# A hybrid decoder trunk on one core: the RWKV chunk inverse kept in SBUF, its blocks moved by 32 by 32 transposes on VectorE and joined on TensorE, and one norm's two partial sums in the other order

## The chip, the cores and the metric

The kernel runs on one core of one Trainium2 chip. The metric is device time in microseconds (us) of one execution. TensorE is called PE here, VectorE DVE, ScalarE ACT, GpSimd POOL; SP is the engine that issues most DMAs. PE's clock has two levels, 1.2 and 2.4 GHz; a granted clock of 1.00 in a row is the upper one.

## The reference, cut to what matters

The model has two layers. Each is a half-step SwiGLU network ("FFN0"), a mixer of three parallel branches, and a second half-step SwiGLU ("FFN2"); a normalisation and a modulation by a conditioning vector stand ahead of each. Everything is float32, with 256 tokens and a width of 1024.

```
for l in range(2):
    u = modulate(rms_norm(h, norm_w[l, 0]), m[0], m[1])
    h = h + 0.5 * m[2] * swiglu(u, ffn_w_gate[l, 0], ffn_w_up[l, 0], ffn_w_down[l, 0])
    u = modulate(rms_norm(h, norm_w[l, 1]), m[3], m[4])
    p = u @ w_in[l]            # attention | RWKV-7 | HGRN2 | gates
    y = g_a*(diff_attention(..) @ w_out_a) + g_b*(rwkv7_time_mix(..) @ w_out_b) + g_c*(hgrn2_mix(..) @ w_out_c)
    h = h + m[5] * (y @ w_out)
    (FFN2 as FFN0, with m[6..8])

# RWKV-7, per head (8 heads of 64), token after token:
s_kk  = state @ kk_t
state = state * w_t - outer(s_kk, kk_t * a_t) + outer(v_t, k_t)
out_t = state @ r_t
```

The kernel computes the RWKV recurrence in chunks of 64 tokens. For each of 8 heads and 4 chunks that needs the inverse of a unit triangular 64 by 64 matrix, whose off-diagonal part stands in `H`: 32 inverses in each layer. They are built up from blocks: 16 by 16 diagonal blocks by substitution, then the off-diagonal blocks of 32 by 32, then those of 64 by 64.

## The kernel before, in words

**The stream of weights.** All weights are streamed once, in items of up to 512 KB, by DMAs that SP issues (`raw`). ACT rounds each item to `wh` (L375), DVE makes the remainder `wl = raw - wh` (L376), and PE multiplies three products, wh·uh, wh·ul and wl·uh, in `mm3` (L372) or, for the token-major projections, in `tm_proj` (L952 to L954). Each of `wh` and `wl` has three buffers, and an item's matmuls stand two items behind its split.

**The side work.** RWKV, HGRN2 and attention work is written as generators ("tracks"). Between two items `advance` steps them until the costs that they yield use up the item's budget (a negative yield ends the item's share). A scheduler with priorities (`PRIO`) then makes each engine's fixed order from that. So the side work of every engine stands in one queue with the split of the weights: an instruction of the inverse that takes long on DVE stands ahead of a `wl`, and PE waits for that.

**The inverse**, `rwkv_rest`, once a layer. GpSimd issues DMAs that move the 32 by 32 diagonal blocks from `H` to DRAM (`scrA`) and back as `NT`, one block to a partition: 64 of them, stored twice. Fifteen steps t = 1..15 on DVE (L799, L801) make row t of the inverse `Y` of two 16 by 16 blocks at a time. The off-diagonal 16 by 16 block of each follows in four DVE instructions over 2048 elements a partition (L808, L811, L813, L816), half of the eight-row stripes in partitions 0 to 63, half in 64 to 127. `Y` goes back through DRAM (`scrY`) to `Ys`, and the off-diagonal 32 by 32 blocks of the 64 by 64 matrices are made on PE: `Xa` is a transpose on DVE (L837), 32 matmuls (L841), ACT copies to `Tt` (L843), 32 matmuls (L847), DVE copies to `Ys` (L849). The chunk loop behind it (L859 on) reads `Ys`. HGRN2's levels (L1016 to L1078) wait for the flag `inv`, which this function sets.

**Startup.** Before the first item, `mod_step` makes the modulation one column of 128 after another (DVE L324, `mw`), and from it `zf` (ACT L1366, DVE L1367), its split `zh`, `zl` (ACT L375, DVE L376) and the first matmuls (PE L1376). The first step of the generator `constants` is taken there; its other steps come between items.

**Norm sums.** `z_sums` adds the squares of eight tiles of `h` over partitions: GpSimd has summed the squares of all tiles but the last into `acc` (L422), the last stands in `sq`, and PE multiplies `acc` and then `sq` by ones into one PSUM tile (L433).

Of the kernel before, what the change touches and what calls it, by code (L numbers as in the profile page):

```python
# [10 lines left out]
F32 = mybir.dt.float32  # L11
# [3 lines left out]
AF = mybir.ActivationFunctionType  # L15
# [48 lines left out]
def trunk(ctx: ExitStack, tc: tile.TileContext, A, out):  # L64
# [36 lines left out]
    id32 = cp.tile([128, 32], F32, name="id32")  # L101
    omu = cp.tile([128, L, 15], F32, name="omu")
# [21 lines left out]
    def constants():  # L124
# [26 lines left out]
        for i, n in enumerate(LV):  # L151
# [9 lines left out]
            for r in range(0, 128, 32):  # L161
                GP.tensor_copy(lmask[r:r + 32, i], lmf[r:r + 32, 1, r:r + 32])
            yield 0.1
# [265 lines left out]
    def z_sums():  # L429
        ps = psm([128, 2])  # L430
        for i, sq in enumerate((NOW["acc"], NOW["sq"])):
            for b in range(2):
                PE.matmul(ps[:, b:b + 1], sq[:, b * 128:(b + 1) * 128], ones[:, 0:1],  # L433
                          start=i + b == 0, stop=i + b == 2)
# [114 lines left out]
    scr = drp.tile([2, 2, 16, 32, 32], F32, name="scrA")  # L549
    scy = drp.tile([2, 2, 16, 32, 32], F32, name="scrY")  # L550
# [3 lines left out]
    def mixer(l):  # L554
# [218 lines left out]
        def rwkv_rest():  # L773
# [5 lines left out]
            for q in range(2):  # L779
                for p in range(2):  # L780
                    r0 = 64 * p + 32 * q
# [5 lines left out]
            for d in range(2):  # L787
                GP.dma_start(NT[64 * d:64 * d + 64], scr.rearrange("q p m s t -> (q p m) s t"))
            GP.memset(Y, 0.0)
            GP.memset(Y.rearrange("m a b -> m (a b)")[:, 0:1024:33], 1.0)  # L790
            yield 0.1
# [5 lines left out]
            for t in range(1, 16):  # L797
                tm = TM[:, 0:2 * t * t].rearrange("m (g j s) -> m g j s", g=2, j=t)
                V.tensor_tensor(tm, ap(Y, 0, [[528, 2], [32, t], [1, t]]), ap(NT, t, [[528, 2], [0, t], [32, t]]),  # L799
                                ALU.mult)  # L800
                V.tensor_reduce(ap(Y, t, [[528, 2], [32, t]]), tm, AX.X, ALU.add)  # L801
                yield 0.2 + 4 * t * t / 960.0
            Yh = tile_([128, 8, 16], "Yh", "rnt")
            PT = tile_([128, 8, 16], "PT", "rny")
            V.tensor_copy(Yh[0:64], Y[0:64, 0:8, 0:16])
            V.tensor_copy(Yh[64:128], Y[64:128, 8:16, 0:16])
            tm = TM.rearrange("m (j t s) -> m j t s", j=8, t=16)
# [5 lines left out]
            V.tensor_tensor(tm, PT.unsqueeze(2).to_broadcast([128, 8, 16, 16]),  # L813
                            ap(Y, 528, [[0, 8], [1, 16], [32, 16]]), ALU.mult)
            yield 2.2
            V.tensor_reduce(Yh, tm, AX.X, ALU.add)  # L816
            yield -2.2
            V.tensor_copy(Y[0:64, 0:8, 16:32], Yh[0:64])
            V.tensor_copy(Y[64:128, 8:16, 16:32], Yh[64:128])
            sm = scy.rearrange("q p m s t -> (q p m) s t")  # L820
            GP.dma_start(sm[:, 0:8], Y[0:64, 0:8])
            GP.dma_start(sm[:, 8:16], Y[64:128, 8:16])
# [647 lines left out]
```

## Time and profile before

| | |
|---|---|
| runs shown | 1449.04, 1449.73, 1454.76 us; median 1449.73 |
| the profiled execution | 1454.69 us, of which the span of the profile is 1453.0 |
| mean granted clock of PE over the span | 0.988 |
| PE busy | 1401.6 us, 96% |
| DVE busy | 1184.9 us, 82% |
| ACT busy | 803.3 us, 55% |
| POOL busy | 150.2 us, 10% |

The profile follows one execution. It gives for each engine what ran when and, for each idle stretch, which instruction ended it. Waits are put down to the one that came last. "x8" in a timeline row is a run of eight instructions of one form in succession.

### The profile page before, as it was taken

Reading aid. Unit: us, or ns where it says so; the run is one execution under the profiler, and the core shown is the slowest. Engines: PE = TensorE matmul, PEld = TensorE weight load, DVE = VectorE, ACT = ScalarE, POOL = GpSimd, SP = SyncE. Lnnn points to the kernel's source line nnn. Section 1 sums busy time; section 2 is a strip of 40 time slices with the busy share of each in tenths; the row PEclk is TensorE's granted clock in tenths of the full one; section 3 lists DMA queues with packets and bytes.
Section 4 is the critical chain, followed back from the end, with each engine's and each line's share of the span. In section 5 each row is a group of like instructions: output and inputs, shape, how many; then the busy total and the mean of one; then the engine's idle time right before and its main releaser. Section 6 shows DMA issues by size and latency. Waiting matters only on the chain. (4 is left out here: it accounts for less than half of the span.)

```text
span 1453.0 us, 31223 instructions
## 1 busy us (share of the span) xinstructions
PE 1401.6 (96%) x12420; PEld 1331.2 (92%) x12420; DVE 1184.9 (82%) x2216; ACT 803.3 (55%) x1374; POOL 150.2 (10%) x251
## 2 busy tenths in 40 slices
PE   4999999999899999999999999999989999999999
PEld 3899999998678899999999999999877789999998
DVE  5999988869679999888879898787797788886553
ACT  2575447874255646554545544588534664665542
POOL 6200010031310021000000000100322001100000
PEclk9999999999799999999999999999999999999999
DMA  9769984455415657899878998544552235665564
GB/s 358 264 241 362 322 311 167 146 160 163 130 60 178 201 183 264 291 332 319 303 251 296 351 344 299 191 143 144 182 165 78 76 129 174 202 220 192 198 194 127
DMA packets 90370, 316.51 MB, mean 218 GB/s; under 512 B 10608, under 2 KB 13040, under 8 KB 90224
## 3 DMA queue, kind: packets, MB, share of 16 engines
q1 hardware_dynamic: 86832, 308.84, 62.0%
q0 software_dynamic: 1600, 4.20, 1.1%
q8 instruction: 97, 1.59, 0.4%
q10 hardware_dynamic: 1792, 1.48, 0.4%
q14 instruction: 49, 0.40, 0.1%
HBM read 312.38 MB, written 2.10 MB: 216 GB/s over the span
## 5 line engine op out<-in xcount | busy, mean ns | idle before, releaser
L375 ACT CAST wh<-raw 128x1024 fp32r<-128x1024 f32 (+1 forms) x440 | 455.5, 1036 | 426.9 <-PE psd L372 237.3
L376 DVE TENSOR_TENSOR wl<-raw,wh 128x1024 fp32r<-128x1024 f32 (+1 forms) x440 | 537.2, 1222 | 110.7 <-ACT wh L375 106.6
L372 PE MATMUL psd<-uh,wl 128*128 128x256 f32 x1664 | 228.9, 279 | 6.5 <-DVE wl L376 6.5
L372 PE MATMUL psd<-uh,wh 128*128 128x256 f32 x1664 | 231.4, 280 | 0.0
L372 PE MATMUL psd<-ul,wh 128*128 128x256 f32 x1664 | 227.1, 278 | 0.0
L372 PEld LDWEIGHTS psd<-uh,wl 128*128 128x128 f32 x1664 | 207.2, 189 | 8.2 <-DVE wl L376 7.7
L372 PEld LDWEIGHTS psd<-uh,wh 128*128 128x128 f32 x1664 | 207.7, 188 | 5.0 <-issue 2.7
L372 PEld LDWEIGHTS psd<-ul,wh 128*128 128x128 f32 x1664 | 206.4, 188 | 0.4
L324 DVE SCALAR_TENSOR_TENSOR mw<-mw,cbc 128x1024 f32<-128x1024 f32 x134 | 168.2, 1257 | 1.7 <-DMA mw<-in_modw 1.6
L372 PE MATMUL psd<-hl,wh 128*128 128x256 f32 x704 | 96.8, 278 | 0.0
L372 PE MATMUL psd<-hh,wl 128*128 128x256 f32 x704 | 96.6, 278 | 0.0
L372 PE MATMUL psd<-hh,wh 128*128 128x256 f32 x704 | 96.3, 277 | 0.0
L422 POOL TENSOR_TENSOR acc<-acc,sq 128x256 f32<-128x256 f32 x36 | 31.1, 865 | 575.1 <-ACT sq L420 443.6
L372 PEld LDWEIGHTS psd<-hl,wh 128*128 128x128 f32 x704 | 87.9, 188 | 0.0
L372 PEld LDWEIGHTS psd<-hh,wl 128*128 128x128 f32 x704 | 87.9, 188 | 0.0
L372 PEld LDWEIGHTS psd<-hh,wh 128*128 128x128 f32 x704 | 87.7, 188 | 0.0
L953 PE MATMUL psd<-wl,uh 128*128 128x512 f32 x160 | 66.5, 416 | 3.8 <-DVE wl L376 3.8
L954 PE MATMUL psd<-wh,ul 128*128 128x512 f32 x160 | 67.3, 421 | 0.0
L952 PE MATMUL psd<-wh,uh 128*128 128x512 f32 x160 | 66.0, 414 | 0.0
L372 PE MATMUL psd<-zh,wh 128*128 128x258 f32 x448 | 65.2, 286 | 0.0
L372 PE MATMUL psd<-zh,wl 128*128 128x258 f32 x448 | 64.9, 283 | 0.0
L372 PE MATMUL psd<-zl,wh 128*128 128x258 f32 x448 | 63.9, 283 | 0.0
(428 smaller groups left out, 2032.3 us busy)
## 6 DMA issues: line engine op xcount, KB each, us to landing
raw<-in_gu SPq DMA_DIRECT2D x176, 512.0 KB, 4.7
mw<-in_modw SPq DMA_DIRECT2D x134, 512.0 KB, 5.5
raw<-in_wfm SPq DMA_DIRECT2D x94, 512.0 KB, 3.3
raw<-in_dn SPq DMA_DIRECT2D x64, 512.0 KB, 4.7
raw<-in_wtm SPq DMA_DIRECT2D x40, 512.0 KB, 3.3
raw<-in_dn SPq DMA_DIRECT2D x32, 384.0 KB, 4.4
raw<-in_wo SPq DMA_DIRECT2D x24, 512.0 KB, 3.3
raw<-in_wout SPq DMA_DIRECT2D x16, 512.0 KB, 3.3
```

Source lines behind the costliest of these rows:

```text
L324: ins = V.scalar_tensor_tensor(w, w, 1.0, NOW["cbc"], ALU.mult, ALU.mult, accum_out=modd[:, l, j, f:f + 1])
L372: PE.matmul(p, w[:, sl[k]], xs[k][x], start=first and i == 0, stop=last and i == 3 * n - 1)
L375: SC.copy(dst_h, src)
L376: V.tensor_sub(dst_l, src, dst_h.bitcast(F32))
L422: GP.tensor_add(NOW["acc"], NOW["acc"], sq)
L952: PE.matmul(ps[b], u[k][0][:, ts_], w1, start=k == 0, stop=False)
L953: PE.matmul(ps[b], u[k][0][:, ts_], w2, start=False, stop=False)
L954: PE.matmul(ps[b], u[k][1][:, ts_], w1, start=False, stop=k == KT - 1)
```

## The change

The change keeps the inverse in SBUF and has these parts.

1. `Hd` collects the 32 by 32 diagonal blocks of `H` by four copies (two ACT, two POOL). One DVE transpose of 32 by 32 squares (128x512, `To`) puts each column of a block in a partition, so that with scaling by a mask each of the 128 partitions holds one 16 by 16 block in `NT`.
2. The mask `half` (1 in the partitions of the second halves of the squares, and its complement) is made once, in `constants`, from `lmf`: two DVE instructions in the pass n = 16.
3. The fifteen steps work on one 16 by 16 block a partition, so on t·t elements instead of 2·t·t.
4. A second transpose puts `Y` back, two ACT instructions with the mask make the block-diagonal `Yd`, and a third transpose makes `Xa`. The off-diagonal 16 by 16 blocks are made on PE: two groups of 64 matmuls of 32 by 32, on the four tile positions (32i, 32i), with an ACT copy (`Tt`) between them and a DVE addition behind. Copies (two ACT, two POOL) put the result in `Ys`, and a fourth transpose makes `Xa` for the 64 by 64 step.
5. The 64 by 64 step stays, but its two groups run over m outside and p inside, so that two tile positions alternate.
6. The yield costs differ, and `scrA`, `scrY`, the 2048-element tile and 12 DMAs a layer are gone.
7. `z_sums` multiplies `sq` first and `acc` second.

```diff
+            if n == 16:
+
+                V.tensor_reduce(half[:, 0:1], lmf[:, 1], AX.X, ALU.max)
+                V.tensor_scalar(half[:, 1:2], half[:, 0:1], -1.0, 1.0, ALU.mult, ALU.add)
             yield 0.1
...
-        for i, sq in enumerate((NOW["acc"], NOW["sq"])):
+        for i, sq in enumerate((NOW["sq"], NOW["acc"])):
...
-                    GP.dma_start(scr[q, p].rearrange("m s t -> s m t"),
-                                 H[r0:r0 + 32, :, :, 32 * q:32 * q + 32].rearrange("s j c t -> s (j c) t"))
-            NT = tile_([128, 32, 32], "NT", "r")
-            Y = tile_([128, 32, 32], "Y", "k")
-            TM = hp.tile([128, 2048], F32, name="TM", tag="ZH")
...
+            quad = [slice(32 * i, 32 * i + 32) for i in range(4)]
+            Hd = tile_([128, 16, 32], "Hd", "Xa")
+            for i, r in enumerate(quad):
+                (GP.tensor_copy if i % 2 else SC.copy)(
+                    Hd[r].rearrange("s (j c) t -> s j c t", j=4), H[r, :, :, 32 * (i % 2):32 * (i % 2) + 32])
+            yield -0.1
...
+            To = tile_([128, 16, 32], "To", "Tt")
+            V.transpose(To.rearrange("p t (g m) -> p t g m", g=2), Hd.rearrange("p m (g t) -> p t g m", g=2))
+            GP.memset(Bd[:, :, 0:16], 0.0)
+            SC.activation(Bd[:, :, 16:32], Hd[:, :, 16:32], AF.Copy, scale=half[:, 0:1])
+            yield -0.7
+            SC.activation(NT, To[:, :, 0:16].rearrange("p t s -> p s t"), AF.Copy, scale=half[:, 0:1])
+            V.scalar_tensor_tensor(NT, To[:, :, 16:32].rearrange("p t s -> p s t"), half[:, 1:2], NT, ALU.mult, ALU.add)
+            yield -0.4
...
             for t in range(1, 16):
-                tm = TM[:, 0:2 * t * t].rearrange("m (g j s) -> m g j s", g=2, j=t)
...
-                yield 0.2 + 4 * t * t / 960.0
...
-            V.tensor_tensor(tm, Yh.unsqueeze(2).to_broadcast([128, 8, 16, 16]),
-                            ap(NT, 16, [[0, 8], [1, 16], [32, 16]]), ALU.mult)
-            yield 2.2
-            V.tensor_reduce(PT, tm, AX.X, ALU.add)
-            yield 2.2
...
+                tm = TM[:, 0:t * t].rearrange("m (j s) -> m j s", j=t)
+                V.tensor_tensor(tm, ap(Y, 0, [[16, t], [1, t]]), ap(NT, t, [[0, t], [16, t]]), ALU.mult)
+                V.tensor_reduce(ap(Y, t, [[16, t]]), tm, AX.X, ALU.add)
+                yield 0.4 + 2.7 * t * t / 960.0
+            To = tile_([128, 16, 32], "To", "Tt")
+            V.transpose(To.rearrange("p t (g m) -> p t g m", g=2),
+                        Y.rearrange("p s t -> p t s").unsqueeze(2).to_broadcast([128, 16, 2, 16]))
             M["inv"] = True
-            yield 0.255
-
+            yield -0.7
+            for g in range(2):
+                SC.activation(Yd[:, :, 16 * g:16 * g + 16], To[:, :, 16 * g:16 * g + 16].rearrange("p t m -> p m t"),
+                              AF.Copy, scale=half[:, g:g + 1])
+            yield -0.1
             Xa = tile_([128, 16, 32], "Xa")
             Tt = tile_([128, 16, 32], "Tt")
             p1 = psm([128, 16, 32])
+            V.transpose(Xa, Yd)
+            yield -0.6
+            for m in range(16):
+                for i, r in enumerate(quad):
+                    PE.matmul(p1[r, m], Bd[r, m], Xa[r, m], start=True, stop=True, tile_position=(32 * i, 32 * i))
+            SC.copy(Tt, p1)
+            yield -0.2
+            p2 = psm([128, 16, 32])
+            for m in range(16):
+                for i, r in enumerate(quad):
+                    PE.matmul(p2[r, m], Tt[r, m], Yd[r, m], start=True, stop=True, tile_position=(32 * i, 32 * i))
+            V.tensor_tensor(Yd[:, :, 16:32], Yd[:, :, 16:32], p2[:, :, 16:32], ALU.add)
+            for i, r in enumerate(quad):
+                (GP.tensor_copy if i % 2 else SC.copy)(Ys[r, :, 32 * (i % 2):32 * (i % 2) + 32], Yd[r])
+            V.transpose(Xa, Yd)
+            yield -1.0
...
-            for p, (a_, b_) in enumerate(hv):
-                for m in range(16):
+            for m in range(16):
+                for p, (a_, b_) in enumerate(hv):
                     PE.matmul(p1[b_, m], H[a_, m // 4, m % 4, 32:64], Xa[a_, m], start=True, stop=True,
                               tile_position=(64 * p, 64 * p + 32))
```

Three places show how instructions move. A row of these lists is an engine's own order: line, operation, tiles, shape of the result, and how many in succession.

**DVE, startup, from the second column of the modulation on.** The weighted column `mw` (L324 before, L329 now), `zf` (L1367, now L1377) and the remainder `zl` (L376, now L381) are the chain to the first matmuls. Before:

```order
L324 SCALAR_TENSOR_TENSOR mw,modd<-mw,cbc 128x1024
L340 TENSOR_TENSOR mods<-modd,cols 128x1
L1367 COPY zf<-mods 128x2
L376 TENSOR_TENSOR zl<-zf,zh 128x258
L324 SCALAR_TENSOR_TENSOR mw,modd<-mw,cbc 128x1024
L328 TENSOR_SCALAR modd<-modd,mb_105,cols 128x1
```

And now:

```order
L329 SCALAR_TENSOR_TENSOR mw,modd<-mw,cbc 128x1024
L345 TENSOR_TENSOR mods<-modd,cols 128x1
L1377 COPY zf<-mods 128x2
L166 TENSOR_REDUCE half<-lmf 128x1
L167 TENSOR_SCALAR half<-half 128x1
L173 TENSOR_SCALAR omu<-cols 128x15
L381 TENSOR_TENSOR zl<-zf,zh 128x258
L175 TENSOR_SCALAR hka<-cols 128x4
...
L187 TENSOR_TENSOR hm<-hm,cols 128x4
L329 SCALAR_TENSOR_TENSOR mw,modd<-mw,cbc 128x1024
```

The reduction to `half`, and behind it twelve small constants of the same generator (`omu` to `hm`), now stand ahead of the next `mw`; before, these constants (L168 to L202) stood in FFN0.

**PE, layer 0, where the inverse's matmuls stand.** L952 to L954 (now L962 to L964) and L372 (now L377) are weight items, L1016 (now L1026) is HGRN2. Before:

```order
L841 MATMUL psm<-Xa,H 32x32 x16
L954 MATMUL psd<-wh,ul_3047 128x512
...
L841 MATMUL psm<-Xa,H 32x32 x16
L847 MATMUL psm<-Ys,Tt 32x32 x16
L1016 MATMUL psm<-hw,hk 32x32 x28
L847 MATMUL psm<-Ys,Tt 32x32 x16
L1016 MATMUL psm<-hw,hk 32x32 x4
L864 MATMUL psm<-SV,Za 64x64 x4
```

And now, where each "..." behind an L377 row stands for the rest of 24 L377 matmuls, one weight item:

```order
L1026 MATMUL psm<-hw,hk 32x32 x32
L831 MATMUL psm<-Xa,AI 32x32 x64
L377 MATMUL psd<-uh_2897,wh 128x256
...
L837 MATMUL psm<-AI,Tt 32x32 x64
L1026 MATMUL psm<-hw 32x32 x32
L377 MATMUL psd<-uh_2897,wh 128x256
...
L849 MATMUL psm<-Xa,H 32x32 x32
L377 MATMUL psd<-uh_2897,wh 128x256
...
L856 MATMUL psm<-AI,Tt 32x32 x32
L1026 MATMUL psm<-hw 32x32 x32
```

The groups of the inverse now stand apart, with one item of 24 large matmuls between each and the next, and the first of them stands some 190 rows of PE's order earlier than the first L841 stood.

**PE, the end of a layer's output projection, at the norm's sums** (L433 before, L438 now; `yl`, `yh` belong to the projection, `zh` to the next network). Before:

```order
L372 MATMUL psd<-yl_6743,wh 128x256
L433 MATMUL psm<-ones,acc 128x1 x2
L372 MATMUL psd<-yl_6762,wh 128x256
...
L372 MATMUL psd<-zh,wh 128x258 x7
L372 MATMUL psd<-zh,wl 128x258 x6
L433 MATMUL psm<-ones,sq 128x1 x2
L372 MATMUL psd<-zh,wl 128x258
```

And now:

```order
L377 MATMUL psd<-yh_6891,wl 128x256
L377 MATMUL psd<-zh,wh 128x258 x7
L377 MATMUL psd<-zh,wl 128x258 x6
L438 MATMUL psm<-ones,sq 128x1 x2
L438 MATMUL psm<-ones,acc 128x1 x2
L377 MATMUL psd<-zh,wl 128x258
```

The product with `acc` stood inside the stream of the items before; now both stand where only `sq` stood. This is so at the five places where `z_sums` follows a stream of items.

## Rows read from the trace of the kernel before

**Rows 1.** The page, part 1: busy us (share of the span) xinstructions of each engine.

```profile
PE 1401.6 (96%) x12420; PEld 1331.2 (92%) x12420; DVE 1184.9 (82%) x2216; ACT 803.3 (55%) x1374; POOL 150.2 (10%) x251
```

**Rows 2.** Windows: us, busy (x) by engine, granted clock of PE, DMA share, GB/s.

```profile
355.00:370.00 15.00, 9.91 (x77) 9.00 (x76) 14.97 (x10) 4.69 (x9) 3.81 (x6) 0.98 0.36 123
370.00:380.00 10.00, 8.97 (x60) 7.04 (x60) 7.68 (x10) 3.92 (x6) 5.56 (x7) 0.84 0.66 201
380.00:397.00 17.00, 17.00 (x314) 14.00 (x312) 8.84 (x15) 4.20 (x7) 1.77 (x3) 0.51 0.34 107
398.00:420.00 22.00, 22.00 (x441) 17.81 (x440) 17.30 (x32) 12.47 (x24) 8.23 (x8) 1.00 0.16 51
1066.00:1083.00 17.00, 12.86 (x72) 11.02 (x71) 16.94 (x15) 5.23 (x8) 5.64 (x9) 0.80 0.44 137
1093.00:1100.00 7.00, 6.81 (x70) 5.08 (x66) 2.87 (x6) 1.05 (x2) 0.52 (x1) 0.51 0.28 105
```

**Rows 3.** Waits: engine, tile, line <- releaser: us in total, times, longest.

```profile
PE psd L1376 <- DVE zf L1367: 13.9, 4, 11.5
...
PE psd L372 <- DVE wl L376: 6.5, 6, 2.0
...
PE psm L433 <- POOL acc L422: 4.4, 5, 1.6
...
PE psd L953 <- DVE wl L376: 3.8, 3, 1.9
...
PE psm L841 <- DVE Xa L837: 2.1, 3, 1.0
```

**Rows 4.** Timeline of DVE: start, us, instruction [idle before <- releaser].

```profile
352.82 4.04 DVE L808 TENSOR_TENSOR TM<-Yh,NT 128x2048 f32<-128x2048 f32 x1
```

**Rows 5.** Timeline of PE: a wait for wl in the inverse, and one outside it.

```profile
358.05 1.21 PE L372 MATMUL psd<-uh,wl 128*128 128x256 f32 x8 [0.97 <-DVE wl L376]
...
463.67 0.50 PE L953 MATMUL psd<-wl,uh 128*128 128x512 f32 x1 [1.09 <-DVE wl L376]
```

**Rows 6.** Groups by line: count | busy, mean ns of one | idle before.

```profile
L808 DVE TENSOR_TENSOR TM<-Yh,NT 128x2048 f32<-128x2048 f32 x2 | 8.1, 4044 | 0.0
...
L813 DVE TENSOR_TENSOR TM<-PT,Y 128x2048 f32<-128x2048 f32 x2 | 7.9, 3926 | 0.0
```

**Rows 7.** Timeline of DVE behind the inverse.

```profile
371.19 0.68 DVE L1062 TENSOR_TENSOR hw<-hw,hq 128x512 f32<-128x512 f32 x1
...
377.33 0.70 DVE L837 STREAM_TRANSPOSE Xa<-Ys 32x512 f32<-32x512 f32 x1 [0.51 <-DMA Ys<-scrY]
```

**Rows 8.** Timeline of PE at four groups of small matmuls.

```profile
345.14 1.07 PE L372 MATMUL psd<-uh,wl 128*128 128x256 f32 x8
346.14 0.76 PE L1016 MATMUL psm<-hq,hk 128*32 128x32 f32 x64
346.83 1.18 PE L372 MATMUL psd<-uh,wh 128*128 128x256 f32 x8
...
400.31 0.68 PE L873 MATMUL psm<-R,Ys 64*64 64x64 f32 x16
...
1087.64 1.17 PE L841 MATMUL psm<-Xa,H 32*32 32x32 f32 x32 [0.69 <-DVE Xa L837]
```

**Rows 9.** Timeline of POOL in the startup, the masks.

```profile
16.28 1.24 POOL L138 TENSOR_SCALAR_AFFINE_SELECT mpos<-mpos 64x64 f32<-64x64 f32 x1
...
18.60 0.24 POOL L136 TENSOR_SCALAR_AFFINE_SELECT mneg<-mneg 64x64 f32<-64x64 f32 x1
...
27.12 1.40 POOL L158 TENSOR_SCALAR_AFFINE_SELECT lmf<-lmf 128x128 f32<-128x128 f32 x1
```

**Rows 10.** Timeline of DVE in the startup, and in FFN0.

```profile
21.33 0.43 DVE L376 TENSOR_TENSOR zl<-zf,zh 128x258 fp32r<-128x258 f32 x1 [3.52 <-ACT zh L375]
21.68 1.22 DVE L324 SCALAR_TENSOR_TENSOR mw<-mw,cbc 128x1024 f32<-128x1024 f32 x1
...
66.11 0.17 DVE L168 TENSOR_SCALAR omu<-cols 128x15 f32<-128x15 f32 x1
```

More of the change, by code (lines that the diff above doesn't have):

```diff
@@ L101, in trunk @@
     id32 = cp.tile([128, 32], F32, name="id32")
+    half = cp.tile([128, 2], F32, name="half")
     omu = cp.tile([128, L, 15], F32, name="omu")
@@ L777, in rwkv_rest @@
                 GP.memset(Ys[64 * p + 32:64 * p + 64, :, 0:32], 0.0)
-            for q in range(2):
-                for p in range(2):
-                    r0 = 64 * p + 32 * q
-                    GP.dma_start(scr[q, p].rearrange("m s t -> s m t"),
-                                 H[r0:r0 + 32, :, :, 32 * q:32 * q + 32].rearrange("s j c t -> s (j c) t"))
-            NT = tile_([128, 32, 32], "NT", "r")
-            Y = tile_([128, 32, 32], "Y", "k")
-            TM = hp.tile([128, 2048], F32, name="TM", tag="ZH")
-            for d in range(2):
-                GP.dma_start(NT[64 * d:64 * d + 64], scr.rearrange("q p m s t -> (q p m) s t"))
-            GP.memset(Y, 0.0)
-            GP.memset(Y.rearrange("m a b -> m (a b)")[:, 0:1024:33], 1.0)
-            yield 0.1
+            quad = [slice(32 * i, 32 * i + 32) for i in range(4)]
[4 more added lines that the diff above has]
+            yield -0.1
+            NT = tile_([128, 16, 16], "NT", "r")
+            Y = tile_([128, 16, 16], "Y", "k")
+            TM = tile_([128, 256], "TM", "rnt")
+            AI = tile_([128, 2, 16, 32], "AI", "a")
+            Bd, Yd = AI[:, 0], AI[:, 1]
+            GP.memset(Y, 0.0)
+            GP.memset(Y.rearrange("m a b -> m (a b)")[:, 0:256:17], 1.0)
+            To = tile_([128, 16, 32], "To", "Tt")
[6 more added lines that the diff above has]
+            yield -0.4
             def ap(t, off, dims):
@@ L815, in rwkv_rest @@
[L815 to L822, printed above, removed]
-            GP.dma_start(sm[:, 16:32], Y[0:64, 16:32])
-            for q in range(2):
-                for p in range(2):
-                    r0 = 64 * p + 32 * q
-                    GP.dma_start(Ys[r0:r0 + 32, :, 32 * q:32 * q + 32], scy[q, p].rearrange("m s t -> s m t"))
@@ L833, in rwkv_rest @@
             p1 = psm([128, 16, 32])
+            V.transpose(Xa, Yd)
[14 more added lines that the diff above has]
+            yield -1.0
+            p1 = psm([128, 16, 32])
             p2 = psm([128, 16, 32])
             hv = [(slice(64 * p, 64 * p + 32), slice(64 * p + 32, 64 * p + 64)) for p in range(2)]
-            for a_, b_ in hv:
-                V.transpose(Xa[a_], Ys[a_, :, 0:32])
-            yield -1.2
-            for p, (a_, b_) in enumerate(hv):
-                for m in range(16):
+            for m in range(16):
+                for p, (a_, b_) in enumerate(hv):
                     PE.matmul(p1[b_, m], H[a_, m // 4, m % 4, 32:64], Xa[a_, m], start=True, stop=True,
                               tile_position=(64 * p, 64 * p + 32))
+            for p, (a_, b_) in enumerate(hv):
                 SC.copy(Tt[b_], p1[b_])
             yield -0.2
+            for m in range(16):
+                for p, (a_, b_) in enumerate(hv):
+                    PE.matmul(p2[a_, m], Tt[b_, m], Yd[b_, m], start=True, stop=True,
+                              tile_position=(64 * p + 32, 64 * p))
             for p, (a_, b_) in enumerate(hv):
-                for m in range(16):
-                    PE.matmul(p2[a_, m], Tt[b_, m], Ys[b_, m, 32:64], start=True, stop=True,
-                              tile_position=(64 * p + 32, 64 * p))
                 V.tensor_copy(Ys[a_, :, 32:64], p2[a_])
```

12 lines of the change are left out of this document (removed).

## The prediction, made before the result was known

> **What bounds the kernel now.** First the busy times of the page: PE is busy for 1401.6 of 1453.0 us, the next engine, DVE, for 1184.9 [rows 1]. So PE sets the end, and DVE's or POOL's freed time is worth nothing by itself. A change can give time only in three ways: it removes waits of PE, it removes stretches in which PE runs at the lower clock, or it shortens PE's own work. PE's idle time is 51 us. The list of waits then shows whose they are [rows 3]: 13.9 us for `zf`, almost all in the startup, 10.3 us for `wl` (6.5 and 3.8), 4.4 us for `acc` in `z_sums`, 2.1 us for the inverse's `Xa`.
>
> Third, the place of those for `wl`. DVE's timeline shows a 4.04 us instruction of the inverse (L808) at 352.82 us, with the split of a weight item behind it [rows 4]; PE waits 0.97 us for that split at 358.05 us [rows 5]. All waits for `wl` but the one of 1.09 us at 463.67 us [rows 5] lie at the inverse, four in each layer. So the inverse costs PE 10.3 - 1.1 + 2.1 = 11.3 us of waits.
>
> Fourth, the windows of the same stretches, for the clock [rows 2]. In 355:370 PE is idle for 5.09 us at granted clock 0.98; then the clock is 0.84, and 0.51 in 380:397. In layer 1 it is 0.80 in 1066:1083, with 4.14 us idle, and 0.51 in 1093:1100. A stretch of length T at mean clock c holds 2(1-c)T at the lower level of 1.2 GHz: 3.2 + 16.7 us in layer 0, 6.8 + 6.9 us in layer 1, 34 us in all. The fall comes behind idle time; in 398:420, where PE is busy throughout, the clock is 1.00, although 441 instructions there, most of them small, run with it. So I put the fall down to the idle time, not to the small matmuls.
>
> **The change, part by part.** The profiled execution took 1454.7 us, 0.3% above the median of 1449.73 and just under the slowest of the three runs shown, so part of the gain below may be missing in a run that had less of the slow clock.
>
> *The waits at the inverse: -11.3.* The four long DVE instructions are gone (L808 and L813 take 4.04 and 3.93 us a piece [rows 6]). What DVE has in their place is four transposes a layer: the one of 32x512 takes 0.70 us [rows 7]; other 128x512 operations take 0.68 [rows 7], so I take 0.7 for 128 partitions, and at worst four times that, 2.8, which is still under L808. The fifteen steps work on half the elements. No DVE instruction longer than `wl`'s own (some 1.2 us) is left.
>
> *New waits: +2.* PE's order shows that the four groups of the inverse stand an item of 24 L377 matmuls apart. Three runs of eight at 1.07 us [rows 8] give some 3 us of cover to each hand-over: ACT copy, matmuls, DVE addition, transpose. A layer's waits for `Xa` were 2.1/2 us [rows 3]; I take half of that and as much again for a `wl` behind a transpose: 1 us a layer, 2 us in all. Without the cover each hand-over would cost its own length, some 2 us, 8 us a layer.
>
> *The clock: -14.* If the waits go, the slow stretches go. Of 34 us at half speed, with the idle parts of these windows out, some 31 are work that would take half: 15.7. I take 14, since the remaining waits may bring a short fall. Bounds: 0 (the fall has another cause) and 16.
>
> *PE's own small matmuls: +2, and group changes: +1.* Each layer gets 128 more small matmuls, two records each in the trace, so 256. L1016 on four tile positions takes 0.76 us for 64 records, 11.9 ns each; L841 on one position at a time takes 1.17 for 32, 36.6 ns each [rows 8]. The new groups rotate over four positions, as L1016: 256 x 11.9 = 3.0 us. The old two groups (128 records) now alternate between two positions. The nearest row for that is L873: 16 records in 0.68 us with two positions [rows 8], by length of a row 0.58 of what one at a time would take. So 128 x 36.6 = 4.7 us becomes 2.7. Net +1.0 a layer, +2. Upper bound, all at 36.6 ns and nothing saved: +9.4 a layer. Changing between forms: eight L372 behind L1016 take 1.18 instead of 1.07 [rows 8]; three more changes a layer, with both edges, give about 0.5, so +1.
>
> A rule stands against this part. The Trainium skill, "TensorEngine Tiling (Array Packing)", section "Restrictions and Gotchas", says that different row tiles must write to different PSUM banks, since they can't access one at the same time; `p1` is one PSUM tile written by four row tiles. By that rule the new groups would run one after another: some +17 us instead of +2. Row L873 speaks against it: there two row tiles write into one PSUM tile, and take less than L841's rate would give.
>
> *`z_sums`: -4.4.* PE waited five times for POOL's `acc`, 4.4 us, the longest 1.6 [rows 3], because the two products with `acc` had been moved into the stream ahead. Now they stand behind `sq`, which is made after `acc`'s last addend, and `acc` is covered by some 13 L377 matmuls more. The cover gone (POOL later than `sq`) it costs up to the same 4.4 again.
>
> *The startup: +7.* This part of the change doesn't look like one. `half` is a DVE reduction of `lmf`, which POOL makes. In DVE's order it now stands ahead of `zl` and of the next `mw`, in the chain that PE waits for. Before, `zl` ran at 21.33 us and `mw` at 21.68 [rows 10], while `lmf` was done only at 27.12 + 1.40 = 28.5 us [rows 9]. It will come sooner than that: POOL is slow beside a running DVE (a 64x64 mask select takes 1.24 us at 16.28 and 0.24 at 18.60, when DVE waits [rows 9, 10]) and DVE will now stand still. Three such slow instructions of about 1 us each lie ahead, so I estimate 25.2. DVE then does the reduction, `omu`, `zl` and ten constants, and the next `mw` comes at 27.1 instead of 21.68: +5.4. The other constants that were in FFN0 (0.17 us at 66.11 [rows 10], a new one every 0.08) now follow between the first columns: about twenty, +1.6. PE can't absorb that, for it waits for `zf` in this chain already [rows 3], and DVE has hardly a pause in it. Bounds: 5.4 (constants hidden) and 10.3 (`lmf` at 28.5 as before, the rest behind it).
>
> *The rest at nothing.* ACT's new copies and scalings stand ahead of `wh`; ACT is busy for 55% [rows 1]. In 355:397 it is busy for 12.8 of 42 us [rows 2], so they fit; were that cover gone, some six at about 0.6 us would delay `wl` by 3.6 us a layer. The DRAM trip saves PE only the `Xa` wait counted above, and POOL's freed DMA issues serve nobody.
>
> Sum: 1454.7 - 11.3 + 2 - 14 + 2 + 1 - 4.4 + 7 = 1437.0.
>
> **The rivals.**
>
> *R1, the startup costs little.* If POOL gets `lmf` done by about 21 us, or PE catches up later, the term is 0 to 2 instead of 7: about 1431. Against it: POOL had six instructions and `lmf`'s two selects still ahead at 21.7.
>
> *R2, the new chain has waits of its own.* Six ACT instructions, four transposes and four hand-overs stand in the queues of the splits. If each hand-over is late by 1 us, 4 to 5 us a layer, and a short slow stretch comes with it: +9, 1446. For it: the chain is longer in steps than before. Against it: the 24 matmuls between.
>
> *R3, the new groups run serially*, as the page's rule would have it. Then 256 x 36.6 = 9.4 us in place of 3.0, and 4.7 in place of 2.7: +8.4 a layer, 1437 + 17 = 1454, no change.
>
> *R4, slower: the clock stays low through the whole spread stage.* The small groups now stand between large ones over some 240 rows of PE's order in each layer, about 45 us. If it is the alternation with small groups that lowers the clock (0.51 in 380:397 with 314 instructions [rows 2]) and not the idle time before it, all that is at 1.2 GHz. Without any lower clock the sum is 1437 - 2 = 1435; x us of slow stretch add x/2. It decides for slower beyond x = 44 us (1457). With 90 us it gives 1480. Against it: 398:420 at 1.00 [rows 2].
>
> **How the numbers follow.** Forecast 0.66, with its own range 1430 to 1442 (startup 5.4 to 10.3, clock and waits a few us either way); R1 0.09; R2 0.13; R3 0.06; R4 0.06. The predicted time is 1437, 0.9% below the median. Leaving out R3 and R4 and the outer ends of R1 and R2 gives 1428 to 1446. A measurement of this kernel can tell about 0.5% from no change: below 1442.5 is faster, above 1457.0 slower. Faster: forecast 0.63, R1 0.09, R2's lower part 0.03, together 0.75. Slower: R4 and a little of R3, 0.07. The rest, 0.18, is within.
>
> **What would show it right or wrong.** In the profile after, DVE's timeline must show `half` waiting for `lmf` until about 25 us, and PE's first long run of matmuls some 7 us later. The list of waits must have no PE wait for `acc` and at most some 2 us for `wl` and `Xa`; the windows at the inverse must show granted clock 1.00. A group L831 of 64 matmuls (128 records) must take about 1.5 us; 4.7 would mean R3. The prediction is wrong if the clock there is near 0.5 without idle time ahead (R4), if PE waits for `Tt` or `Xa` between the groups (R2), or if startup has moved by less than 3 us (R1).

## The result, and the profile after

| | before | after |
|---|---|---|
| median of 9 runs each, us | 1452.47 (1449.04 to 1458.38) | 1442.51 (1438.03 to 1446.32) |
| ratio, 95% interval | | 0.9934 [0.9917, 0.9952] |
| profiled execution, us (span) | 1454.69 (1453.0) | 1445.27 (1443.6) |

Faster by 0.66%, inside the range that was given; the forecast was 0.9%. The page of the changed kernel first: part 1 answers to [rows 1], and of part 3 one queue is shown (packets, MB, share).

```profile
span 1443.6 us, 32223 instructions
...
PE 1390.0 (96%) x12932; PEld 1323.8 (92%) x12932; DVE 1159.7 (80%) x2210; ACT 810.4 (56%) x1392; POOL 140.5 (10%) x235
...
q8 instruction: 101, 1.65, 0.5%
```

PE still sets the end. It is idle for 1443.6 - 1390.0 = 53.6 us, before for 1453.0 - 1401.6 = 51.4 [rows 1]: the change as a whole removed no idle time, and its gain lies in PE's busy time, which is 11.6 us shorter. The list of waits after (total us, times, longest) answers to [rows 3]:

```profile
PE psd L1386 <- DVE zf L1377: 13.8, 3, 11.9
...
PE psm L1026 <- issue: 5.9, 2, 3.0
PE psd L963 <- DVE wl L381: 5.9, 7, 1.8
PE psd L1386 <- DVE hs L193: 5.4, 1, 5.4
PE psm L874 <- DVE SV L901: 2.2, 2, 1.1
...
PE psd L377 <- DVE wl L381: 1.8, 1, 1.8
...
PE psm L438 <- ACT sq L425: 1.1, 1, 1.1
```

`acc` and `Xa` are gone, and `wl` has fallen from 10.3 to 7.7 us. New are 5.9 us of "issue" ahead of L1026 (a wait for nothing that the profile shows), 2.2 us for `SV`, and 5.4 us for `hs`, one of the small constants that stand in the startup now. In PE's timeline at the inverse of layer 0 (start, duration, a run of x records) one of the two "issue" waits is seen:

```profile
343.09 0.50 PE L963 MATMUL psd<-wl,uh 128*128 128x512 f32 x1 [1.35 <-DVE wl L381]
...
349.26 1.29 PE L831 MATMUL psm<-Xa,AI 32*32 32x32 f32 x128
...
353.51 1.29 PE L837 MATMUL psm<-AI,Tt 32*32 32x32 f32 x128
354.73 0.32 PE L1026 MATMUL psm<-hw 128*32 128x32 f32 x13
357.89 0.96 PE L1026 MATMUL psm<-hw 128*32 128x32 f32 x51 [2.84 <-issue]
```

The four-position groups take 1.29 us for 128 records, 10.1 ns each. Then PE stops for 2.84 us in the middle of a group whose operands are there: 13 of its 64 records lie ahead of the pause, 51 behind. The windows (as [rows 2]) show where the granted clock is under 1.00:

```profile
28.00:40.00 12.00, 8.24 (x20) 6.17 (x21) 10.68 (x43) 2.92 (x7) 10.72 (x24) 0.57 0.81 267
355.00:370.00 15.00, 12.16 (x297) 11.66 (x292) 6.37 (x9) 6.42 (x11) 3.75 (x5) 0.77 0.28 93
455.00:470.00 15.00, 11.39 (x40) 8.97 (x40) 14.91 (x42) 4.58 (x5) 0.00 (x0) 0.77 0.74 241
560.00:575.00 15.00, 13.87 (x102) 13.61 (x101) 11.99 (x33) 8.00 (x12) 0.74 (x1) 0.89 0.82 288
1060.00:1075.00 15.00, 11.95 (x370) 11.35 (x357) 7.49 (x11) 6.71 (x11) 4.10 (x5) 0.89 0.31 108
```

By 2(1-c)T that is 10.3 + 6.9 + 6.9 + 3.3 + 3.3 = 30.7 us at 1.2 GHz, where before had 34, all of it at the inverse. At the inverse 10.2 us are left; 20.5 have appeared elsewhere, each behind idle time (constants in the startup, `wl` at 456 to 460 us, `sq` at 562.8 us). Not every wait has such a stretch behind it: behind the 1.35 us at 343.09 the clock stays at 1.00.

The startup, on DVE:

```profile
17.96 0.17 DVE L1377 COPY zf<-mods 128x2 f32<-128x2 f32 x1
...
25.11 0.28 DVE L166 TENSOR_REDUCE half<-lmf 128x1 f32<-128x128 f32 x1 [6.99 <-POOL lmf L159]
...
25.58 0.42 DVE L381 TENSOR_TENSOR zl<-zf,zh 128x258 fp32r<-128x258 f32 x1
...
26.94 1.33 DVE L329 SCALAR_TENSOR_TENSOR mw<-mw,cbc 128x1024 f32<-128x1024 f32 x1
```

DVE stands still for 6.99 us, until POOL has `lmf`, with `zl` and `mw` queued behind; in [rows 10] the same `mw` started at 21.68. POOL gains by it: its last select ahead of `half` takes 0.33 us, where before it took 1.40 beside a running DVE [rows 9].

```profile
24.75 0.33 POOL L159 TENSOR_SCALAR_AFFINE_SELECT lmf<-lmf 128x128 f32<-128x128 f32 x1
```

PE's first run of projection matmuls in before, and then in after, with PE's wait for the constants ahead of it:

```profile
50.33 0.84 PE L372 MATMUL psd<-zh,wh 128*128 128x258 f32 x4
```

```profile
30.39 3.78 PE L1386 MATMUL psd<-zf,raw 128*128 128x258 f32 x8 [5.36 <-DVE hs L193]
...
56.95 0.71 PE L377 MATMUL psd<-zh,wh 128*128 128x258 f32 x3
```

**Where the 9.4 us of the two profiles lie.** Setting the start of the k-th large matmul (L372 and L952 to L954, now L377 and L962 to L964; 9888 in each trace) of one trace against that of the other gives the lead at every place: +6.6 us at the start; -4.0 between 104 and 230 us; -1.4, -3.0, -1.4, -1.6 and -1.2 at the five norm sums, -8.6 together; -1.1 across the spread stage with the inverse in layer 0 and -5.5 in layer 1; +2.9 at the slow clock of 565 us. They add up to -9.7; the last large matmul has -9.4.

### The profile page after: what moved, and what is told of

It reads as the page before. It is cut to its first block, busy times and chain, and to the rows that moved or that the text cites. A ratio compares the mean times of both kernels' runs of the same rounds, so it can differ in the third digit from the quotient of the medians.

```text
span 1443.6 us, 32223 instructions
## 1 busy us (share of the span) xinstructions
PE 1390.0 (96%) x12932; PEld 1323.8 (92%) x12932; DVE 1159.7 (80%) x2210; ACT 810.4 (56%) x1392; POOL 140.5 (10%) x235
## 3 DMA queue, kind: packets, MB, share of 16 engines
q0 software_dynamic: 544, 1.58, 0.3%
## 4 chain that ended last, share of the span: by engine, by line
PE 77%; DVE 11%; ACT 7%; issue 3%; DMA 1%; POOL 1%; ACTq 0%; DVEq 0%; POOLq 0%
PE psd L377 65%; DVE wl L381 3%; ACT wh L380 2%; PE psd L963 1%; PE psd L962 1%; PE psd L964 1%; DMA h<-in_x 1%; DVE TM L812 1%; DVE mw L329 1%; PE psd L1386 1%; ACT ae L1216 1%; PE psm L1026 1%; PE psm L678 0%; PE psm L752 0%; PE psm L906 0%
## 5 line engine op out<-in xcount | busy, mean ns | idle before, releaser
L381 DVE TENSOR_TENSOR wl<-raw,wh 128x1024 fp32r<-128x1024 f32 (+1 forms) x440 | 535.0, 1217 | 128.8 <-ACT wh L380 108.7
L377 PE MATMUL psd<-uh,wh 128*128 128x256 f32 x1664 | 234.0, 282 | 0.0
L377 PE MATMUL psd<-uh,wl 128*128 128x256 f32 x1664 | 227.5, 278 | 1.8 <-DVE wl L381 1.8
L377 PE MATMUL psd<-ul,wh 128*128 128x256 f32 x1664 | 228.3, 278 | 0.0
L377 PEld LDWEIGHTS psd<-uh,wh 128*128 128x128 f32 x1664 | 208.7, 189 | 5.2 <-issue 2.0
L377 PEld LDWEIGHTS psd<-uh,wl 128*128 128x128 f32 x1664 | 206.7, 189 | 3.1 <-DVE wl L381 2.2
L377 PEld LDWEIGHTS psd<-ul,wh 128*128 128x128 f32 x1664 | 207.0, 189 | 0.5
L329 DVE SCALAR_TENSOR_TENSOR mw<-mw,cbc 128x1024 f32<-128x1024 f32 x134 | 167.3, 1250 | 1.8 <-DMA mw<-in_modw 1.7
L377 PE MATMUL psd<-hh,wh 128*128 128x256 f32 x704 | 95.4, 276 | 0.0
L377 PE MATMUL psd<-hl,wh 128*128 128x256 f32 x704 | 95.4, 276 | 0.0
L377 PE MATMUL psd<-hh,wl 128*128 128x256 f32 x704 | 95.4, 276 | 0.0
L377 PEld LDWEIGHTS psd<-hh,wh 128*128 128x128 f32 x704 | 86.9, 188 | 0.0
L377 PEld LDWEIGHTS psd<-hl,wh 128*128 128x128 f32 x704 | 86.9, 188 | 0.0
L377 PEld LDWEIGHTS psd<-hh,wl 128*128 128x128 f32 x704 | 86.9, 188 | 0.0
L377 PE MATMUL psd<-zh,wh 128*128 128x258 f32 x448 | 66.1, 289 | 0.0
L377 PE MATMUL psd<-zh,wl 128*128 128x258 f32 x448 | 64.9, 283 | 0.0
L962 PE MATMUL psd<-wh,uh 128*128 128x512 f32 x160 | 64.8, 407 | 0.0
L377 PE MATMUL psd<-zl,wh 128*128 128x258 f32 x448 | 64.7, 286 | 0.0
L964 PE MATMUL psd<-wh,ul 128*128 128x512 f32 x160 | 64.7, 404 | 0.0
```

The costliest lines, as they stand in the source:

```text
L329: ins = V.scalar_tensor_tensor(w, w, 1.0, NOW["cbc"], ALU.mult, ALU.mult, accum_out=modd[:, l, j, f:f + 1])
L377: PE.matmul(p, w[:, sl[k]], xs[k][x], start=first and i == 0, stop=last and i == 3 * n - 1)
L381: V.tensor_sub(dst_l, src, dst_h.bitcast(F32))
L962: PE.matmul(ps[b], u[k][0][:, ts_], w1, start=k == 0, stop=False)
L964: PE.matmul(ps[b], u[k][1][:, ts_], w1, start=False, stop=k == KT - 1)
```

## The experiments

Each is compared with the kernel before, run on the same chip.

**1. The startup alone.** `half` is made by POOL, in three instructions, and DVE doesn't wait.

```diff
-                V.tensor_reduce(half[:, 0:1], lmf[:, 1], AX.X, ALU.max)
-                V.tensor_scalar(half[:, 1:2], half[:, 0:1], -1.0, 1.0, ALU.mult, ALU.add)
+                GP.tensor_add(half, lmf[:, 1, 16:64:32], lmf[:, 1, 80:128:32])
+                GP.tensor_add(half[:, 0:1], half[:, 0:1], half[:, 1:2])
+                GP.tensor_scalar(half[:, 1:2], half[:, 0:1], -1.0, 1.0, ALU.mult, ALU.add)
```

(The section on the change says that `half` is 1 in the second halves of the squares of 32; `lmf` gives 1 to the first sixteen partitions of each. For the time it is the same.)

> The change with one edit: the mask half is made by three small GpSimd instructions instead of a DVE reduction, so that DVE's order in the startup is again that of before. If the startup costs what the trace after shows (the first projection matmuls at 56.95 us instead of 50.33), they return to about 50.3 us and the time falls by about 6.6 us against the changed kernel, from 1442.5 to about 1436, ratio to before about 0.989. The rival, that the startup's delay is taken up later by waits that vanish, gives a time within 2 us of the changed kernel's, ratio about 0.993.

Measured: 1439.22 (1432.26 to 1443.56), ratio 0.9917 [0.9884, 0.9950]. Its timelines of DVE, and of PE, have the start where before had it:

```profile
21.59 1.22 DVE L330 SCALAR_TENSOR_TENSOR mw<-mw,cbc 128x1024 f32<-128x1024 f32 x1
```

```profile
50.36 0.84 PE L378 MATMUL psd<-zh,wh 128*128 128x258 f32 x4
```

So the reduction's place in DVE's queue costs the 6.6 us at the first matmul. In the two traces 5.1 us of this lead are left at the last large matmul; by medians 3.3 us come back at the end, by the ratios 2.5. The time lies between the two that were expected, the intervals of the two ratios overlap, and how much of the 6.6 us reaches the end isn't resolved.

This trace also has a stretch at the lower level without idle time ahead of it, in windows on both sides of 424 us:

```profile
396.00:420.00 24.00, 24.00 (x244) 20.53 (x242) 10.28 (x24) 10.54 (x22) 0.00 (x0) 1.00 0.29 91
420.00:424.00 4.00, 4.00 (x19) 2.20 (x18) 3.85 (x12) 3.36 (x7) 0.00 (x0) 1.00 0.37 125
424.00:432.00 8.00, 8.00 (x34) 5.49 (x35) 4.59 (x21) 2.41 (x7) 0.00 (x0) 0.58 0.21 66
```

PE is busy from 396 us on, with fewer records from 420 us, and the clock falls to 0.58. So idle time isn't all that goes ahead of a fall; what else does, no run shows.

**2. The norm sums, from both sides.** One kernel is the change with the old order of the two products, the other is the kernel before with the new order.

```diff
-        for i, sq in enumerate((NOW["sq"], NOW["acc"])):
+        for i, sq in enumerate((NOW["acc"], NOW["sq"])):
```

> The change with z_sums in the old order, acc first. If the new order is worth the 4.4 us of waits that the trace before shows, PE waits again for acc five times, about 4 us in all, and the time is about 1446 to 1447, ratio 0.996. If PE would only wait a moment later for sq, the time stays at 1442.5 and the sum of waits of the L438 matmuls is about the same in both.

Measured: 1449.11, ratio 0.9987 [0.9968, 1.0007]: without this line the change is worth nothing that can be told. Its list of waits has `acc` again:

```profile
PE psm L438 <- POOL acc L427: 5.3, 5, 2.3
```

> The kernel before with one edit: z_sums with sq first and acc second. If the order is worth the 4.4 us of waits for acc, the time is 1447, ratio 0.997, and the list of waits shows at most some 1 us for sq in their place. It is also a second look at the old inverse: the waits for wl and Xa at the inverse should be 11 us again, and the half clock some 25 to 35 us; if the half clock of the profile before was an outlier, it is 15 us or less here.

Measured: 1442.97, ratio 0.9953 [0.9938, 0.9968], 6.8 us faster than before with this line alone. That is more than the 4.4 us of waits. At such a place of before, in PE's timeline, the two products with `acc` form a group of their own, and its own length goes too:

```profile
740.55 0.61 PE L433 MATMUL psm<-ones,acc 128*128 128x1 f32 x4 [0.72 <-POOL acc L422]
```

Here the large matmuls gain 1.4 us, about 0.72 + 0.61. The second question of that run is answered too: with the old inverse PE spends some 31 us at the lower level again, so the 34 of the profile before were no outlier.

**3. The pause without a releaser.** The theory: PE has no instructions. PE takes one instruction for each matmul record and one for each weight load; in the page these are 2 x 12932 after and 2 x 12420 before [rows 1]. Divided by 256 that gives 101.0 and 97.0, and the queue `q8 instruction` moved 101 and 97 packets of 16 KB. So a packet is a block of 256 instructions, 128 records. The rival: something at this place of the program (a PSUM tile, POOL's copies) holds PE. The first test puts 32 matmuls that nobody reads (64 records) far ahead of the place. If blocks are the cause, the pause must move against the program.

```diff
     def z_rstd():
+        if "dummy" not in NOW:
+            NOW["dummy"] = dm = psm([128, 32])
+            for i in range(32):
+                PE.matmul(dm[0:32], ones[0:32, 0:32], ones[0:32, 0:32], start=True, stop=True)
```

> The changed kernel with 32 extra 32 by 32 matmuls (64 records, each with its weight load, so 128 instructions) in the startup, whose result nothing reads; PE's order is otherwise the same. It tells what the 2.8 and 3.1 us of idle PE in the middle of an L1026 group are. If PE runs out of instructions, which arrive in blocks of 256, the idle time moves with the block's edge: by 64 records towards earlier, out of the L1026 group into the L837 group ahead of it, in both layers. If it hangs on these instructions (their operands, their PSUM tile, the form), it stays at record 13 or 14 of the L1026 group.

Measured in a single run: 1445.2 us, and q8 moved 102 packets. The two pauses are 5.6 us together. The one of layer 0 now stands inside the first group of the inverse, a group earlier than expected, and a small one follows it:

```profile
350.69 0.76 PE L1030 MATMUL psm<-hw,hk 128*32 128x32 f32 x64
351.38 1.05 PE L835 MATMUL psm<-Xa,AI 32*32 32x32 f32 x100
355.46 0.44 PE L835 MATMUL psm<-Xa,AI 32*32 32x32 f32 x28 [3.03 <-issue]
...
364.33 0.74 PE L377 MATMUL psd<-ul,wh 128*128 128x256 f32 x4 [0.47 <-issue]
```

Counted from the start of the L1026 group ahead of the inverse, the pause of after came at record 64 + 128 + 24 + 128 + 13 = 357, this one at 64 + 100 = 164: 193 earlier, that is the 64 records put in and one block of 128 (and one record). Counted from the start of the program, the pauses of after come behind 2889 and 9380 of PE's records, those of this run behind 2760 and 9251, and its two small ones (0.9 us together) behind 3016 and 9507: all in a layer are whole blocks of 128 apart, to one record. The rival falls.

**4. The groups further apart**, with three more yields between them.

```diff
             SC.copy(Tt, p1)
             yield -0.2
+            yield -0.2
+            yield -0.2
...
             V.transpose(Xa, Yd)
             yield -1.0
+            yield -0.2
```

> The change with two more steps between the first and the second group of the inverse and one more ahead of the third, so that 48 and 48 large matmuls and other small groups stand between them instead of 24. If PE runs out of instructions because too many small ones stand in some 15 us, the idle time of 5.9 us in the L1026 groups falls to under 2 us, with the half clock behind it, and the time falls by 5 to 9 us, to about 1435. If the idle time is bound to the hand-over of these groups, it stays, and the time is 1442.

Measured: 1443.63, ratio 0.9953 [0.9934, 0.9972]. The pauses stay, 6.2 us: the expectation failed. Where one stands says why:

```profile
358.73 1.29 PE L839 MATMUL psm<-AI,Tt 32*32 32x32 f32 x128
359.94 0.45 PE L1029 MATMUL psm<-hw 128*32 128x32 f32 x29
363.42 0.51 PE L1029 MATMUL psm<-hw 128*32 128x32 f32 x35 [3.03 <-issue]
```

It is at record 64 + 128 + 24 + 64 + 48 + 128 + 29 = 485 = 357 + 128, exactly one block on. A group is itself 128 records, a whole block, and PE uses it up in 1.3 us however far the next group is. The pauses come behind 3017 and 9507 records, whole blocks from those of after, to one record.

**5. The row tiles one after other**: the two loops of the new groups are swapped, so that each position does its 16 matmuls before the next one begins.

```diff
-            for m in range(16):
-                for i, r in enumerate(quad):
+            for i, r in enumerate(quad):
+                for m in range(16):
```

> The changed kernel with the two loops of the first two groups (L831, L837) exchanged: all 16 blocks of one tile position, then the next, the same 64 matmuls a group. If it is the alternation of the four positions that makes them fast, a group of 128 records takes 4.7 us (36.6 ns each, as the old L841) instead of 1.29. And if PE's idle time of 5.9 us comes from 256 instructions being used up in under some 4 us, it is gone, since 128 records then take 4.7 us: the span grows by 4 x 3.4 - 5.9, about 7 to 8 us. If the idle time is not that, it stays, and the span grows by about 13 us.

Measured in a single run: 1444.77 us (span 1443.1, after 1443.6). A group takes 3.93 us, 30.7 ns a record, and PE's timeline has no pause:

```profile
357.19 3.93 PE L837 MATMUL psm<-AI,Tt 32*32 32x32 f32 x128
361.06 0.76 PE L1026 MATMUL psm<-hw 128*32 128x32 f32 x64
```

Four groups cost 4 x 2.64 = 10.6 us more, and yet the span is 0.5 us shorter, where 7 to 8 us more were expected. The 5.9 us of pauses are gone, and with them part of the slow clock: some 24 us at the lower level instead of 30.7, worth 3.4. The 2 us that are still missing lie within what single runs of one kernel differ by. So the work of the four row tiles of the change overlaps (10.1 against 30.7 ns a record), and just that speed empties the block.

**6. The groups in halves**, on top of experiment 1: one weight item is let in after half of each group, so that a block holds some 64 fast records and an item of large ones.

```diff
             for m in range(16):
+                if m and m % 8 == 0:
+                    yield -0.2
                 for i, r in enumerate(quad):
```

> The kernel with the mask on GpSimd, and the first two groups of the inverse cut in halves of 32 matmuls with an item of 24 large matmuls between. If the idle time comes from blocks of 256 instructions that are used up too fast, it falls from 5.9 us to some 0 to 4 us, since most blocks now hold 24 large matmuls (2.7 us), and the time falls to between 1433 and 1437, ratio 0.987 to 0.990. If blocks are not the cause, the idle time stays at about 6 us and the time at 1439.

Measured: 1429.09 (1427.83 to 1431.80), ratio 0.9855 [0.9837, 0.9874], 10 us under experiment 1 by the medians, 9 by the ratios. That is below the 1433 to 1437 that were expected. The list of waits of PE has no "issue" any more, and the mean granted clock is 0.998 instead of 0.993. Not all of the gain is that of the pauses: the order of the work behind the inverse has moved too, and the two waits for `wl` near 455 us, 3.1 us in experiment 1, are one of 1.6.

**7. POOL beside DVE**, on top of experiment 6. In after PE waits 1.35 us at 343.09 for a `wl` that took 2.31 us, while POOL multiplies `hgw` (timelines of DVE and of POOL; the mean of this `wl` is 1.22):

```profile
339.59 1.21 DVE L812 TENSOR_TENSOR TM<-Y,NT 128x196 f32<-128x196 f32 x1
340.73 2.31 DVE L381 TENSOR_TENSOR wl<-raw,wh 128x1024 fp32r<-128x1024 f32 x1
```

```profile
339.16 2.80 POOL L1002 TENSOR_TENSOR hgw<-hgw,rows 128x512 f32<-128x512 f32 x2 [12.31 <-DVE hgw L1001]
```

```diff
-                GP.tensor_mul(h4(gw[:, b]), h4(gw[:, b]),
+                V.tensor_mul(h4(gw[:, b]), h4(gw[:, b]),
```

> As groups_in_halves, and HGRN2's gate multiplication hgw (two GpSimd instructions of 1.4 us a layer) on DVE. If the late wl ahead of the inverse (1.35 us of PE's wait a layer, where wl takes 2.31 instead of 1.21 us and L812 1.21 instead of 0.56 beside the GpSimd instructions) is due to GpSimd working at the same time, that wait falls to under 0.5 us, and the time by 1 to 3 us. If DVE is simply too full there, the two added instructions of about 0.7 us make the wait longer.

Measured: 1426.83, ratio 0.9845 [0.9820, 0.9870]. That `wl`, PE's wait at this place and the windows around the two inverses:

```profile
334.54 1.22 DVE L382 TENSOR_TENSOR wl<-raw,wh 128x1024 fp32r<-128x1024 f32 x1
```

```profile
335.82 0.51 PE L968 MATMUL psd<-wl,uh 128*128 128x512 f32 x1 [0.35 <-DVE wl L382]
```

```profile
320.00:400.00 80.00, 78.48 (x1373) 66.38 (x1371) 61.84 (x99) 42.16 (x69) 15.63 (x15) 1.00 0.44 144
1015.00:1095.00 80.00, 78.49 (x1387) 66.32 (x1386) 61.84 (x100) 42.89 (x70) 14.93 (x14) 1.00 0.44 144
```

The waits of L968 for `wl` fall from 5.8 us in experiment 6 to 3.6 (0.7 us of "issue" are back), PE is idle for 1.5 us in each 80, and the clock is 1.00 with all small groups in place. The 2.3 us between the medians of experiments 6 and 7 lie inside their intervals.

**8. Four us that don't belong to the change.** Between 130 and 200 us after runs 620 matmul records and before 596, both with PE always busy at granted clock 1.00. The new tile `half` moves the tiles behind it, which is taken to be by 32 bytes; no view shows their places. Theory: the place of the tiles sets the rate; rival: the execution does. In three kernels a tile that nobody uses is put in: in the kernel before, in that of experiment 7, and in the kernel before with the new order of the norm sums, which also shows the old inverse beside the new one:

```diff
+    gap = cp.tile([128, 2], F32, name="gap")
+    V.memset(gap, 0.0)
```

> The kernel before with one small tile more (128 partitions by 8 bytes, written once and read by nothing) where the change puts half, so that every tile behind it stands 32 bytes further on, as in the change; the order of all engines is the same but for that one write. In the profiles of the two kernels with the old places PE does 596 large matmuls in 130:200 us at granted clock 1.00, in all eight with the new places 620. If the place in SBUF makes that (with the DMA engines 0.95 busy there), this kernel does 620 and gains some 4 us, ratio 0.997. If it comes from anything else of the change, it does 596 and the time stays at 1451.

> The kernel with halves and hgw on DVE, and one more such small tile, so that the tiles stand at the old remainder by 64 bytes (32) again. If the remainder decides, it does 596 large matmuls in 130:200 us and loses some 4 us, from 1426.8 to 1431. If it does not, it does 620 and stays at 1427.

> The kernel before with z_sums in the new order and the tiles 32 bytes further on: all of the change but the inverse. Against it the kernel with half on GpSimd (1439.2) shows what the new inverse is worth as it stands, and the kernel with halves and hgw on DVE (1426.8) what it is worth when its instructions are spread. If the parts add up (6.8 us for z_sums, 4 us for the place), the time is 1440, so that the inverse as it stands gives about 1 us, and spread about 13. If z_sums and place share their gain, the time is 1443.

> The kernel before itself, profiled once more. If PE's lower rate at granted clock 1.00 belongs to the places of the tiles, it does 596 large matmuls in 130:200 us again. If it belongs to an execution, it may do 620 here, and the 4 us are no part of what the change brings.

Measured: the moved kernel before 1448.91, ratio 1.000 [0.9982, 1.0017]; the moved experiment 7 1424.93, ratio 0.9833 [0.9804, 0.9862], the fastest of all; the old inverse with the new norm sums 1441.09, ratio 0.9946 [0.9923, 0.9969]. All three did 620 records in the window, the moved experiment 7 too, for which the theory said 596; and the moved kernel before gained nothing by it. The unchanged kernel before, profiled once more, ran 1452.36 us. Its window, below the one of the profile of before:

```profile
130.00:200.00 70.00, 70.00 (x596) 70.00 (x596) 64.85 (x99) 33.98 (x49) 4.74 (x4) 1.00 0.94 345
```

```profile
130.00:200.00 70.00, 70.00 (x620) 70.00 (x619) 67.52 (x103) 35.81 (x50) 3.61 (x4) 1.00 0.97 358
```

So the same kernel has both rates, and the theory on places falls. The lower rate belongs to an execution, or to something else in which two executions differ, such as the chip; it was in the profile of before (and of the kernel before with the new norm sums, 597) and gave 4.0 us of the 9.4 between the profiles. How often it comes in runs without a profile, and so whether it has a part in the ratio, isn't shown; the 1.000 of the moved kernel is no sign of one. What causes it stays open.

## Why the prediction was right, and which step failed

The time (1437 forecast, 1442.51 measured) lies in the stated range, 1428 to 1446, and 0.5 us outside the forecast's own, 1430 to 1442. It does so partly by luck, through errors of both signs: from the profile of 1454.7 us the sum took 17.7, and the medians differ by 10.0. Of the signs that were to show it right, two failed: the waits for `wl` are 7.7 us and not some 2, and the clock at the inverse is 0.77 and 0.89 and not 1.00.

**Old waits at the inverse, -11.3: right.** The long DVE instructions and the waits for `Xa` are gone, and the waits for `wl` that remain at the inverse stand at other places, for another reason.

**New waits, +2: this step failed.** At the inverse and in the chunk loop they are 12.1 us in the trace. The step counted hand-overs between the groups, and these are hidden as it said: no wait for `Tt` or `Xa` is in the list. What it didn't see are three others: the pauses at block edges, 5.9 us; `wl` ahead of the groups, 0.38 + 0.27 + 1.35 us in layer 0 and 0.39 + 0.25 + 1.37 in layer 1, 4.0 us, of which the longest in a layer falls to 0.35 when POOL's product is taken away (experiment 7); `SV` of the chunk loop, 2.2 us. So R2, at 1446, named the right term with the wrong mechanism. A fourth kind stands behind the inverse and isn't in the 12.1:

```profile
456.96 1.18 PE L377 MATMUL psd<-uh,wl 128*128 128x256 f32 x8 [1.76 <-DVE wl L381]
459.99 0.79 PE L963 MATMUL psd<-wl,uh 128*128 128x512 f32 x1 [1.85 <-DVE wl L381]
```

That is 3.6 us where before had 1.09 [rows 5], with 6.9 us at the lower level behind it. In experiment 7 one wait of 1.58 us is left, at granted clock 1.00. Which part of the change brought the two together isn't shown.

**The clock, -14: right in its cause in the main, far too large.** It was put down to idle time, and a kernel with next to no idle time there has granted clock 1.00 (experiment 7). That idle time is the only cause isn't shown: the fall at 424 us in experiment 1 has none ahead of it. Since the new waits stayed, so did part of the fall. With the startup's 10.3 us set aside (they lie in the startup's term) the profile went from 34 to 20.4 us at 1.2 GHz, which is worth 6.8. Over runs, startup included, the mean clock is 0.988 to 0.990 in three sets of runs of before (14, 17 and 22) and 0.993 in the nine of after: 0.003 to 0.005 of 1445, 5 to 7 us. It is the failed step a second time: behind both block edges stands a slow stretch, in layer 0 of 6.9 us.

**Small matmuls, +2, and group changes, +1: right as far as seen.** L831 and L837 take 1.29 us for 128 records (1.5 forecast). The group changes have no measurement of their own. R3 falls: the groups don't run one after another, which would be the 3.93 us of experiment 5. The rule in the Trainium skill, "TensorEngine Tiling (Array Packing)", section "Restrictions and Gotchas", that different row tiles need different PSUM banks, doesn't show here: four of them write one PSUM tile at 10.1 ns a record.

**`z_sums`, -4.4: mis-sized.** It measured -6.8 us alone (0.9938 to 0.9968, 4.6 to 9.0 us). The term took only the waits; the two products also lost the cost of being a group apart, some 0.6 us at each of five places (seen at one).

**Startup, +7: right, step by step, up to the first projection.** `half` waited until 25.1 us (25.2 forecast), `mw` came at 26.9 (27.1), PE's first projection 6.6 us later. R1's first condition, `lmf` by 21 us, falls; whether PE catches up a part of it later, its second, experiment 1 doesn't resolve. **R4 falls** with experiment 7.

**Together.** The forecast gave the inverse -20.3 us as a whole. In the trace it has -6.6; between kernels that differ in little but the inverse (experiment 1, and the old inverse with the new norm sums) the ratios are 0.9917 and 0.9946, the medians 1439.22 and 1441.09, so 2 to 4 us, which the intervals don't tell from zero. With the groups in halves it is 0.9946 - 0.9855 = 0.0091, 13 us, and with `hgw` moved too 0.9946 - 0.9833 = 0.0113, 16 us: most of the -20 was there, and the new waits, with the slow clock behind them, took it. The account of the two profiles doesn't close: of the 11.6 us by which PE's busy time fell, the clock gives 1.7, the rate of experiment 8 4.0 and the five groups of the norm sums some 3; where the other 3 come from isn't traced.

## What to carry to other kernels

Where an engine always busy is given many very short instructions in a row, count how fast it uses up its instructions, not only what data it waits for, and let long work in among them. A constant that is made "once" is not free if it stands in a queue that something waits for: look at what its producer has still ahead of it. And idle time that is moved isn't removed: here the pauses at 358, 457 to 460, 563 and 1064 us, of 1.1 to 3.6 us, were each followed by 3 to 7 us at the lower clock, while waits of 1.35 us at 343 and 1.12 at 400 us were not.

## What the runs showed of the hardware that was not expected

**PE can run out of instructions.** Blocks of 256 instructions come by a queue of their own, and when the 128 records of one were used up in 1.3 to 1.5 us, PE stood idle at the next edge for 2.4 to 3.3 us, whatever was behind the edge (after, and experiments 1 to 4). Behind a block that took some 2.8 us it was 0.47 us (experiment 3), and at 3.93 us for the 128 records there was no pause (experiment 5). The Trainium skill, "Runtime: NRT & Kernel Launch", section "Instruction fetch mechanics", has the same block, 16 KiB or 256 instructions, and calls the crossing mostly hidden; that holds for this kernel's other edges, and not for these.

**Two rates at one clock.** The same kernel ran 596 or 620 records in the same 70 us at granted clock 1.00, PE busy throughout. No run shows what sets it.

**Row tiles at once.** A record of a 32 by 32 matmul takes 10.1 ns when four positions take turns, and 30.7 ns when one position does 16 matmuls before the next.
